# A decoder layer's FFN opening, its first norm and its buffer addresses rearranged

## The chip, the cores and the metric

The kernel runs on one core of a Trainium2 chip. The metric is device microseconds of one execution; lower is better. The core's engines run their own instruction streams side by side: TensorE (PE; its weight loads are listed as PEld), VectorE (DVE), ScalarE (ACT), GpSimd (POOL) and SyncE (SP, which issues most DMAs).

## The reference

One decoder layer over 512 tokens and 1024 channels, all in float32. Two token mixers work on the same input projection: gated linear attention (a) and sliding-window attention with sinks (b). Their outputs are projected, gated, added and projected by `w_out`; then come a post-norm, a SwiGLU FFN with 2816 hidden channels, and a second post-norm:

```python
def layer_norm(x, g, b):
    mu = jnp.mean(xf, axis=-1, keepdims=True)
    var = jnp.mean(jnp.square(xf - mu), axis=-1, keepdims=True)
    return (xf - mu) * lax.rsqrt(var + LN_EPS) * g + b
...
    merged = jax.nn.sigmoid(g_a) * y_a + jax.nn.sigmoid(g_b) * y_b
    return merged @ w_out
...
        h = layer_norm(DEEPNORM_ALPHA * h + mix, ln1_g[layer], ln1_b[layer])
        ffn = (jax.nn.silu(h @ w_gate) * (h @ w_up)) @ w_down
        h = layer_norm(DEEPNORM_ALPHA * h + ffn, ln2_g[layer], ln2_b[layer])
```

## The kernel before, in words

Every large product is made of three matmuls: each operand is split into a high part in the format fp32r and a low part, the remainder in the same format, and high x high, low x high and high x low are added in PSUM. For a weight, ACT casts the loaded block (`wh<-raw`) and DVE subtracts (`wl<-raw,wh`).

The program goes through these stages, with the times of the profiled execution: input, transposes and the first projections to 30 us; query, key, value and gate projections together with both attentions to 280 (`feat_tile`, line 227, and `gla_values`, line 421); the branch projections and gates to 460 (`pbb`, `pga`, `pba`, line 227); the first 512 columns of `w_out` to 482 (line 768), the second 512, one token tile of 128 after another in `out_half`, to 506 (line 779); norm 1 and the transposes of its result (`turned`, line 800); the FFN to 750; the down projection in two column halves to 876 (line 976); norm 2 and the stores to 885.

Tokens lie in four tiles of 128; `res[t][i]` is the residual of tile t in column half i. `norm_part` adds a result to the residual and takes its statistics. `norm_end` makes, on DVE, (x - mean) * g (line 739, two passes of 512 columns), the reciprocal root with one refining step, and times root plus b (line 751, two more).

The FFN's gate and up projection is one level of a Strassen-like scheme: 7 products in place of 8, for 11 pairs of 256 hidden channels (`i`), gate and up in turn (`n`). Each product ("seventh", line 894) is 12 matmuls of 128x256. The token-side operands are A11 and A12 (the first 256 tokens in two halves of the channels), A22 and the sums S1 to S4, which need all the tokens; `split_cols` (807 and 808) makes a high part on ACT and a low part on a given engine. A product b11 uses A11, b21 uses A12, t1 S1, t2 S2, t3 S3, b22 S4 and t4 A22. The profile calls A operands `a`, S1 to S4 `s`, the PSUM tiles of the products `fx`, `fy`, `fz`, and the weight-side sums `wb` and `wt`; the latter are prepared ahead by `prep_pairs` (ACT casts 880, DVE low parts 881, POOL sums 883 to 888).

The down projection reads for each of 22 hidden blocks `op`, the high and low part of the product act (`piece`, 968 and 969), from 10 buffers. In its second column half, the last 8 blocks are run token tile by token tile, so that each tile's `norm_end` can start when that tile is done.

Buffers come from pools that grow from both ends of SBUF. A pool on the right side ends at the same address and starts where its size puts it. Before, the right pools start at byte 196,576 of a partition (`xparts`: xh and xl, the split input; then `merged`: mh and ml, the split merged branches) or at 188,384 (`sums`: A22 and S1 to S4; then `halves`: op). All these addresses are 32 modulo 64. The tiles of the left pools (weights, A11, A12, and the branch outputs `obh`, `obl`, `oah`, `oal`) start at 0 modulo 64.

The order of the instructions on each engine is set when the program is built: a scheduler simulates the tile graph from the order of the code and issues what it takes to be ready. DMA queues are filled in program order by SP (most loads) and POOL (vectors and residuals).

## Time and profile before

| | us |
|---|---|
| median of 3 runs | 887.66 (887.15 to 888.57) |
| profiled execution | 886.88 |
| its span | 885.1 |
| PE busy | 849.0 (96%) |
| DVE busy | 582.9 (66%) |
| ACT busy | 402.4 (45%) |
| POOL busy | 259.9 (29%) |
| mean granted clock of TensorE | 0.982 |

The span is what the profile shows of the device; the execution's own time is 1.8 us longer. A row of a time line gives start, length, engine, line and operation, the tiles (written <- read), and in brackets the idle time before it with what ended it. Rows of grouped instructions give the count, busy time, mean in ns, and the idle time before them. Matmuls overlap: the distance from start to start, not the length, is what one costs.

### The profile page before, as it was taken

The page shows a single profiled execution, that of the slowest core. Times are in us where ns is not written, and L with a number is a line of the kernel's source. Part 1 is how long each engine was busy: PE and PEld are TensorE (multiplying, and loading weights), DVE is VectorE, ACT ScalarE, POOL GpSimd, SP SyncE. Part 2 cuts the span into 40 slices and gives each one's busy share as a digit, 9 for nine tenths or more (in the row PEclk, how much of TensorE's full clock was granted, in tenths as well). Part 3 has the DMA queues.
Part 4 walks back from the last instruction along what each step waited for, and adds up shares of the span by engine and source line. Part 5 has one row for each costly group of instructions (what it writes and reads, how often), then busy time and mean ns, then how long its engine had stood idle before and what let it go on. Part 6 is the DMA issues. An engine that isn't in the chain of part 4 may idle for free.

```text
span 885.1 us, 12931 instructions
## 1 busy us (share of the span) xinstructions
PE 849.0 (96%) x4922; PEld 729.6 (82%) x4922; DVE 582.9 (66%) x1052; ACT 402.4 (45%) x798; POOL 259.9 (29%) x216
## 2 busy tenths in 40 slices
PE   7999999999999999999999949999999999999995
PEld 6887777777887888888888739999999998788885
DVE  4898887686585533322444998888788789735337
ACT  4557566464553431122332345555554557433421
POOL 3240220112310220000232337555666652521201
PEclk9999999999999999999999968999999999999998
DMA  8423113122122323322229030334444314422202
GB/s 238 143 72 96 49 49 96 49 68 77 48 72 72 95 81 95 102 98 85 96 101 316 3 96 1 96 98 119 112 124 120 100 49 147 139 94 74 95 1 95
DMA packets 92622, 83.16 MB, mean 94 GB/s; under 512 B 4768, under 2 KB 79536, under 8 KB 92560
## 3 DMA queue, kind: packets, MB, share of 16 engines
q1 hardware_dynamic: 90480, 76.89, 29.8%
q0 software_dynamic: 1504, 4.40, 1.4%
q10 hardware_dynamic: 576, 1.05, 0.3%
q8 instruction: 38, 0.62, 0.3%
q14 instruction: 24, 0.20, 0.1%
HBM read 80.23 MB, written 2.10 MB: 93 GB/s over the span
## 4 chain that ended last, share of the span: by engine, by line
PE 68%; issue 13%; POOL 10%; DVE 6%; DMA 2%; ACT 1%; POOLq 0%; SPq 0%; DVEq 0%; ACTq 0%
PE pdn L976 12%; PE pva L421 5%; PE pgb L227 5%; PE pq L227 5%; PE pga L227 5%; PE pr L227 5%; PE pba L227 5%; PE pbb L227 5%; POOL upper L888 3%; POOL upper L885 3%; PE pka L227 3%; PE pw L768 3%; PE pqa L227 3%; POOL upper L886 2%; PE pw L779 2%
## 5 line engine op out<-in xcount | busy, mean ns | idle before, releaser
L160 DVE TENSOR_TENSOR wl<-raw,wh 128x1024 fp32r<-128x1024 f32 x96 | 121.1, 1262 | 147.2 <-ACT wh L159 146.9
L159 ACT CAST wh<-raw 128x1024 fp32r<-128x1024 f32 x96 | 100.5, 1049 | 140.4 <-PE pbb L227 34.3
L976 PE MATMUL pdn<-wh,op 128*128 128x512 f32 (+1 forms) x396 | 112.9, 370 | 2.5 <-ACT op L968 1.6
L881 DVE TENSOR_TENSOR wt<-upper,wt 128x512 fp32r<-128x512 f32 x88 | 77.6, 890 | 32.5 <-ACT wt L880 32.3
L880 ACT CAST wt<-upper 128x512 fp32r<-128x512 f32 x88 | 54.8, 624 | 75.4 <-POOL upper L885 37.2
L976 PEld LDWEIGHTS pdn<-wh,op 128*128 128x128 f32 x396 | 71.2, 188 | 17.5 <-ACT op L968 1.8
L976 PE MATMUL pdn<-wl,op 128*128 128x512 f32 (+1 forms) x198 | 73.2, 370 | 0.0
L894 PE MATMUL fx<-s,wt 128*128 128x256 f32 x528 | 65.9, 280 | 0.0
L894 PEld LDWEIGHTS fx<-s,wt 128*128 128x128 f32 x528 | 64.0, 189 | 0.0
L969 POOL TENSOR_TENSOR op<-act,op 128x512 fp32r<-128x512 f32 x22 | 29.2, 1337 | 81.8 <-ACT op L968 81.8
L883 POOL TENSOR_TENSOR upper<-upper 128x512 f32<-128x512 f32 x22 | 31.6, 1451 | 69.8 <-DVE wb L881 56.6
L695 POOL TENSOR_TENSOR ml<-gb,mh 128x512 fp32r<-128x512 f32 x8 | 11.4, 1423 | 119.7 <-ACT mh L694 119.7
L976 PEld LDWEIGHTS pdn<-wl,op 128*128 128x128 f32 x198 | 37.2, 188 | 6.9
L888 POOL TENSOR_TENSOR upper<-upper,lower 128x512 f32<-128x512 f32 x22 | 33.9, 1540 | 27.6 <-DVE wt L881 25.7
L881 DVE TENSOR_TENSOR wb<-lower,wb 128x512 fp32r<-128x512 f32 x44 | 40.2, 932 | 0.0
L968 ACT CAST op<-act 128x512 fp32r<-128x512 f32 x44 | 26.1, 617 | 25.9 <-PE pdn L976 24.4
L894 PE MATMUL fy<-s,wt 128*128 128x256 f32 x264 | 35.8, 294 | 1.9 <-ACT s L807 1.5
L886 POOL TENSOR_TENSOR upper<-upper,lower 128x512 f32<-128x512 f32 x22 | 36.9, 1695 | 0.1
L894 PEld LDWEIGHTS fy<-s,wt 128*128 128x128 f32 x264 | 34.3, 201 | 2.5 <-ACT s L807 1.9
L894 PE MATMUL fx<-a,wb 128*128 128x256 f32 x264 | 34.0, 283 | 1.1 <-DVE a L808 1.1
L377 ACT ACTIVATE S<-S,nm 128x256 f32<-128x256 f32 (+1 forms) x64 | 30.2, 476 | 10.1 <-DVE es L374 6.0
L894 PE MATMUL fx<-a,wt 128*128 128x256 f32 x264 | 33.5, 282 | 1.0 <-DVE gate L937 0.5
(485 smaller groups left out, 2222.2 us busy)
## 6 DMA issues: line engine op xcount, KB each, us to landing
raw<-in_w_in_dram SPq DMA_DIRECT2D x50, 512.0 KB, 3.7
raw<-in_w_ffn_down_dram SPq DMA_DIRECT2D x22, 512.0 KB, 3.5
upper<-in_w_ffn_gate_dram SPq DMA_DIRECT2D x22, 256.0 KB, 5.5
upper<-in_w_ffn_up_dram SPq DMA_DIRECT2D x22, 256.0 KB, 5.9
lower<-in_w_ffn_gate_dram SPq DMA_DIRECT2D x22, 256.0 KB, 4.9
lower<-in_w_ffn_up_dram SPq DMA_DIRECT2D x22, 256.0 KB, 3.4
raw<-in_w_branch_b_dram SPq DMA_DIRECT2D x8, 512.0 KB, 3.5
raw<-in_w_branch_a_dram SPq DMA_DIRECT2D x8, 512.0 KB, 3.4
```

The lines of the kernel that those rows point to most:

```text
L159: ACT.copy(wh, raw)
L160: DVE.tensor_tensor(wl, raw, wh.bitcast(F32), ALU.subtract)
L227: PE.matmul(ps[:, n0:n1], w, d[k][:, n0:n1] if isinstance(d, list) else d[:, k, n0:n1], start=i == 0, stop=i == 3 * NK - 1)
L377: ACT.activation(S[h], S[h], AF.Exp, bias=nm[:, h : h + 1], accum_out=den[:, h : h + 1])
L421: PE.matmul(pa[c], d[:, k, cs], w, start=k == 0 and i == 0, stop=k == NK - 1 and i == 2)
L880: ACT.copy(w[:, 0], src)
L881: DVE.tensor_tensor(w[:, 1], src, w[:, 0].bitcast(F32), ALU.subtract)
L883: POOL.tensor_tensor(b11, b11, b12, ALU.add)
L886: POOL.tensor_tensor(b12, b12, b22, ALU.add)
L888: POOL.tensor_tensor(b11, b11, b21, ALU.add)
L894: PE.matmul(ps, w[:, x, k * P : (k + 1) * P], op[:, y, k, :], start=start and i == 0, stop=stop and i == len(todo) - 1, skip_group_check=True)
L976: PE.matmul(ps[:, c0:c1], op[:, x, ts], w[y][:, c0:c1], start=start and n == 0, stop=stop and n == 2)
```

## The change

It has five parts.

1. A tile of 32 bytes per partition, `edge`, is put at the outer end of the right side. All right pools now start at 0 modulo 64.
2. `norm_rows` replaces `norm_end` in norm 1: ACT makes (x - mean) * root in two passes, without gain and shift. These are two columns (`lncol`, loaded on POOL's queue at the start) and are applied to the transposed result by `affine`, ACT or DVE, in steps of 128 columns. The residual itself gets them later, by 16 POOL passes (`gain`) in the first half of the down projection; the row vectors g1 and b1 are loaded at the end of the FFN, beside g2 and b2, and no longer before norm 1.
3. The FFN opens with pairs 0 and 1 together: b11 of both, b21 of both, t1 of both and so on. The products that use only the first 256 tokens are then 8, or 96 matmuls, where there were 4. `last_tokens` and `last_sums` make S1 first and the other sums afterwards. Pairs are prepared already between the token tiles of `out_half`; their weights use buffers freed by placing three of the blocks of `w_out` in `four` tiles. The tiles fz move to the other PSUM group.
4. S1, S2 and S3 get a pool of their own, freed after the last pair's t3. The pool `halves` takes its place, with 6 `op` buffers instead of 10, and the first pieces are made before the FFN ends. The low parts of the first column half's pieces are all made by DVE.
5. `wide` has 6 buffers, `four` 11, and the last pair's results share one tile.

```diff
+    edge = tc.alloc_tile_pool(name="edge", bufs=1, side="right")
+    edge.tile([P, 8], F32, tag="edge", name="edge")
     right = phase("xparts", "right")
...
+    for c, v in zip(lncol, (ln1_g, ln1_b)):
+        nc.gpsimd.dma_start(c, v[0].rearrange("(k p) -> p k", p=P))
...
-    gains = [four(n) for n in ("g1", "b1")]
-    for g, v in zip(gains, (ln1_g, ln1_b)):
-        nc.gpsimd.dma_start(g, v.broadcast_to([P, D]))
...
+    def norm_rows(t, stats, name):
+        mv = stat(f"mv{name}{t}", 2)
+        DVE.bn_aggr(mv, stats)
+        y, v, w = stat(f"y{name}{t}", 1), stat(f"v{name}{t}", 1), stat(f"w{name}{t}", 1)
+        ACT.activation(y, mv[:, 1:2], AF.Sqrt, bias=eps)
+        DVE.tensor_scalar(v, mv[:, 1:2], LN_EPS, None, ALU.add)
+        refine(y, v, w)
+        DVE.tensor_scalar(w, mv[:, 0:1], y, -1.0, ALU.mult, ALU.mult)
+        for i in (1, 0):
+            ACT.activation(res[t][i], res[t][i], AF.Identity, bias=w, scale=y)
...
+    def affine(eng, h, cs, pt, kg):
+        for k in range(HK):
+            g, b = [c[:, HK * kg + k : HK * kg + k + 1] for c in lncol]
+            if eng is ACT:
+                ACT.activation(h[:, k, cs], pt[:, k, :], AF.Identity, bias=b, scale=g)
+            else:
+                DVE.tensor_scalar(h[:, k, cs], pt[:, k, :], g, b, ALU.mult, ALU.add)
...
+    def last_tokens(t):
+        cs = slice((t - 2) * P, (t - 1) * P)
+        p22, p21 = turned(t, 1), turned(t, 0)
+        affine(ACT, h22, cs, p22, 1)
+        affine(DVE, s3, cs, p21, 0)
+        DVE.tensor_tensor(s1[:, :, cs], s3[:, :, cs], h22[:, :, cs], ALU.subtract)
         split_cols(S1, cs, s1[:, :, cs], DVE)
...
+    groups = [[0, 1]] + [[i] for i in range(2, HF)]
+    flow = []
+    for grp in groups:
+        order = ORDER if len(grp) == 1 else ["b11", "b21", "t1", "t2", "t3", "b22", "t4"]
+        flow += [(i, q, n) for q in order for i in grp for n in range(2)]
...
+    for t in range(2):
+        out_half(t)
+        norm_rows(t, st1[t][:, 0:2, :], "a")
+        prep_pairs(2 + 2 * t)
+        if t:
+            first_tokens(0)
...
     right.release()
-    right = phase("halves", "right")
+    right = phase("sums", "right")
+    A22, S4 = [operand(right, n) for n in ("a22", "s4")]
+    right2 = phase("sums2", "right")
+    S1, S2, S3 = [operand(right2, n) for n in ("s1", "s2", "s3")]
...
+        if i == done:
+            right2.release()
+            right2 = phase("halves", "right")
...
+                    op = right2.tile([P, 2, T], F32R, tag="op", name=f"op{j}_{k}", bufs=6)
+                    ACT.copy(op[:, 0], act[k])
+                    (POOL if j and k % 2 else DVE).tensor_tensor(op[:, 1], act[k], op[:, 0].bitcast(F32), ALU.subtract)
...
+            for k in range(4):
+                piece(0, k)
...
-            op = right.tile([P, 2, T], F32R, tag="op", name=f"op{j}_{k}", bufs=10)
-            ACT.copy(op[:, 0], act[k])
-            (POOL, DVE)[k % 2].tensor_tensor(op[:, 1], act[k], op[:, 0].bitcast(F32), ALU.subtract)
...
+    g1, b1 = vec_bcast(ln1_g, tail, "g1"), vec_bcast(ln1_b, tail, "b1")
     g2, b2 = vec_bcast(ln2_g, tail, "g2"), vec_bcast(ln2_b, tail, "b2")
...
+        if gain:
+            r, v, op = gain.pop(0)
+            POOL.tensor_tensor(r, r, v, op)
```

The orders below are those of the built programs. A row has the line, the operation, the tile written <- the tiles read with their numbers, the shape, and how often it stands there in a row.

PE before, where the FFN opens: 48 matmuls on A11 and A12 (the last rows of them are shown), then the transposes of token tiles 2 and 3, then t1 on S1.

```order
L894 MATMUL fx_0_4555<-a_4277,wb_0_4575 128x256 x11
L894 MATMUL fx_1_4556<-a_4277,wb_1_4579 128x256 x11
L894 MATMUL fz_0_4559<-a_4278,wb_0_4641 128x256
L894 MATMUL fz_1_4560<-a_4278,wb_1_4644 128x256 x2
L894 MATMUL fz_0_4559<-a_4278,wb_0_4641 128x256 x10
L894 MATMUL fz_1_4560<-a_4278,wb_1_4644 128x256 x10
L800 MATMUL pt_h_1_4478<-ident,res_1_4121 128x128 x4
L800 MATMUL pt_h_0_4485<-ident,res_0_4120 128x128 x4
L800 MATMUL pt_h_1_4518<-ident,res_1_4123 128x128 x4
L800 MATMUL pt_h_0_4525<-ident,res_0_4122 128x128 x4
L894 MATMUL fy_0_4557<-s_4471,wt_0_4595 128x256
L894 MATMUL fy_1_4558<-s_4471,wt_1_4614 128x256
```

PE after, the same place:

```order
L819 MATMUL pt_h_1_4582<-ident,res_1_4129 128x128 x4
L921 MATMUL fx_0_4552<-a_4281,wb_0_4350 128x256 x11
L921 MATMUL fx_1_4567<-a_4281,wb_1_4354 128x256 x11
L819 MATMUL pt_h_0_4587<-ident,res_0_4128 128x128 x4
L921 MATMUL fx_0_4605<-a_4281,wb_0_4399 128x256 x11
L921 MATMUL fx_1_4620<-a_4281,wb_1_4403 128x256 x11
L819 MATMUL pt_h_1_4635<-ident,res_1_4131 128x128 x4
L819 MATMUL pt_h_0_4640<-ident,res_0_4130 128x128 x4
L921 MATMUL fz_0_4659<-a_4282,wb_0_4656 128x256 x12
L921 MATMUL fz_1_4676<-a_4282,wb_1_4673 128x256 x12
L921 MATMUL fz_0_4693<-a_4282,wb_0_4690 128x256 x12
L921 MATMUL fz_1_4710<-a_4282,wb_1_4707 128x256 x12
```

The transposes have moved in among the first products, and four groups of fz, of both pairs, stand behind the last of them and ahead of the first on S1.

DVE after, from the last token tile's shift (L839 is `affine` on DVE, L908 a weight's low part, L859 and L857 `last_sums`, L965 an FFN result) to the low part of S1 (s_4542) for that tile, which is its last row:

```order
L852 TENSOR_TENSOR s1f<-s3f,h_4545 128x4x128
L965 TENSOR_TENSOR act_0_4550<-fz_1_4676,u_01_4580 128x256
L827 TENSOR_TENSOR s_4542<-s1f,s_4542 128x4x128
L908 TENSOR_TENSOR wt_0_4786<-upper_0_4338,wt_0_4786 128x512
L827 TENSOR_TENSOR a_4537<-h_4545,a_4537 128x4x128
L965 TENSOR_TENSOR gate_0_4603<-fz_0_4693,u_10_4618 128x256
L908 TENSOR_TENSOR wt_1_4790<-upper_1_4344,wt_1_4790 128x512
L859 TENSOR_TENSOR s3f<-h_4283,s3f 128x4x128
L965 TENSOR_TENSOR act_0_4550<-fz_1_4710,u_11_4633 128x256
L857 TENSOR_TENSOR s1f<-s1f,h_4283 128x4x128
L908 TENSOR_TENSOR wt_0_4794<-upper_0_4326,wt_0_4794 128x512
L827 TENSOR_TENSOR s_4542<-s1f,s_4542 128x4x128
```

Between the last tile's difference (its L852 row, the first) and that low part stand weight preparations and results of both pairs; before, the four passes L739 and L751 of the last tile stood ahead of it instead.

PE before, in the second half of the down projection, where token tile 0 (pdn_0_0) is finished and tile 1 follows:

```order
L976 MATMUL pdn_0_0_7927<-wh_8184,op_19_8258 128x512 x2
L976 MATMUL pdn_0_0_7927<-wl_8185,op_19_8258 128x512
L976 MATMUL pdn_0_0_7927<-wh_8224,op_20_8264 128x512 x2
L976 MATMUL pdn_0_0_7927<-wl_8225,op_20_8264 128x512
L976 MATMUL pdn_0_0_7927<-wh_8224,op_21_8270 128x512 x2
L976 MATMUL pdn_0_0_7927<-wl_8225,op_21_8270 128x512
L976 MATMUL pdn_1_0_7928<-wh_8100,op_14_8228 128x512 x2
L976 MATMUL pdn_1_0_7928<-wl_8101,op_14_8228 128x512
```

PE after, the last rows of the program:

```order
L1045 MATMUL pdn_3_1_7979<-wh_8272,op_21_8318 128x256
L1045 MATMUL pdn_0_0_7975<-wh_8272,op_21_8318 128x512
L1045 MATMUL pdn_0_0_7975<-wl_8273,op_21_8318 128x512
L1045 MATMUL pdn_1_0_7976<-wh_8272,op_21_8318 128x512
L1045 MATMUL pdn_1_0_7976<-wl_8273,op_21_8318 128x512
L1045 MATMUL pdn_2_0_7977<-wh_8272,op_21_8318 128x512
L1045 MATMUL pdn_2_0_7977<-wl_8273,op_21_8318 128x512
L1045 MATMUL pdn_3_0_7978<-wh_8272,op_21_8318 128x256
L1045 MATMUL pdn_3_0_7978<-wl_8273,op_21_8318 128x256
L1045 MATMUL pdn_3_1_7979<-wh_8272,op_21_8318 128x256
L1045 MATMUL pdn_3_1_7979<-wl_8273,op_21_8318 128x256
```

With 6 buffers, blocks 20 and 21 stand behind blocks 14 to 19 of all four token tiles, and the last block is run for all the tiles in turn.

More of the change, by code (lines that the diff above doesn't have):

```diff
@@ L142, in tile_decoder_layer @@
     NRAW = 3
-    raws, ready = [], []
+    raws, ready, homes = [], [], {}
     def fetch_to(n):
@@ L191, in tile_decoder_layer @@
     gng = const.tile([P, 2], F32, tag="gng", name="gng")
+    lncol = [const.tile([P, NK], F32, tag=f"lncol{i}", name=f"lncol{i}") for i in range(2)]
     sink = const.tile([P, 16], F32, tag="sink", name="sink")
@@ L704, in four @@
     def four(name, dt=F32):
-        return late.tile([P, 1024], dt, tag="four", name=name, bufs=12)
+        return late.tile([P, 1024], dt, tag="four", name=name, bufs=11)
+    first_wo = index["wo", 1][0]
+    for i in range(first_wo + 1, first_wo + 4):
+        homes[i] = four
     def vec_bcast(v, home, tag):
@@ L895, in seventh @@
                       stop=stop and i == len(todo) - 1, skip_group_check=True)
-    act = [[None] * HF for _ in range(2)]
-    act_pairs = [[four(f"act{h}_{p}").rearrange("p (k t) -> p k t", k=2) for p in range((HF + 1) // 2)]
-                 for h in range(2)]
     T0, T1 = slice(0, HT), slice(HT, T)
@@ L957, in tile_decoder_layer @@
     limit[0] = len(units)
[L960 removed]
+    g1, b1 = vec_bcast(ln1_g, tail, "g1"), vec_bcast(ln1_b, tail, "b1")
     g2, b2 = vec_bcast(ln2_g, tail, "g2"), vec_bcast(ln2_b, tail, "b2")
     st2 = new_stats("b")
[L963 to L971 removed]
+    gain = [(r, v[i], op) for t in range(NT) for i, r in enumerate(res[t]) for v, op in ((g1, ALU.mult), (b1, ALU.add))]
     def down(k, t, ps, w, op, start, stop, c0=0, c1=512):
```

172 lines of the change are left out of this document (93 added, 79 removed).

## The prediction

> **What bounds the kernel now.** I read the stretch table first, then the chain, the shapes on TensorE, and the time lines of the places that the change touches. The stretch table gives for each stretch its length, the busy time of PE, PEld, DVE, ACT and POOL, and the granted clock.
>
> ```profile
> 30.00:280.00 250.00, 248.54 (x1295) 196.26 (x1294) 192.64 (x491) 138.83 (x340) 50.27 (x46) 1.00 0.25 70
> 328.00:460.00 132.00, 132.00 (x578) 108.13 (x577) 45.32 (x49) 34.79 (x42) 13.28 (x9) 1.00 0.31 95
> 506.00:549.00 43.00, 28.36 (x191) 26.46 (x190) 38.65 (x58) 23.31 (x44) 22.97 (x15) 0.76 0.19 50
> 549.00:750.00 201.00, 199.53 (x1677) 198.51 (x1675) 168.43 (x241) 111.75 (x238) 107.71 (x73) 1.00 0.37 103
> 750.00:876.00 126.00, 124.08 (x594) 102.27 (x594) 64.49 (x87) 45.90 (x68) 30.79 (x25) 1.00 0.25 84
> 876.00:885.10 9.10, 0.00 (x0) 0.00 (x0) 4.94 (x12) 0.82 (x3) 3.11 (x3) 0.61 0.31 115
> ```
>
> TensorE is the bound in all but two stretches: 506 to 549 (norm 1 into the FFN: DVE 38.65 of 43, PE 28.36 at a clock of 0.76) and the tail after 876. So the change can act in four ways: on the rate of single matmuls, on that transition, on the FFN's end, and on the tail. The chain (start, length) shows the first:
>
> ```profile
> 327.95 43.55 PE pbb L227 x192
> 371.49 44.80 PE pga L227 x192
> 416.30 43.56 PE pba L227 x192
> 459.86 22.39 PE pw L768 x96
> ```
>
> All are 128x512 matmuls without a gap. pbb and pba read oh/ol, at 0 mod 64 bytes: 43.55/192 = 226.8 ns. pga reads xh/xl and pw reads mh/ml, which the program puts at 32 mod 64: 44.80/192 = 233.3 and 22.39/96 = 233.2 ns. The weights are the same kind of tile in all four.
>
> **Part 1, the aligned pools.** By shape (count, busy us, mean ns; the mean overlaps with the next matmul, so only differences count):
>
> ```profile
> L227 PE MATMUL pga<-xh,wh 128*128 128x512 f32 x64 | 25.3, 395 | 0.0
> L227 PE MATMUL pba<-oah,wh 128*128 128x512 f32 x64 | 24.9, 389 | 0.0
> L894 PE MATMUL fx<-s,wt 128*128 128x256 f32 x528 | 65.9, 280 | 0.0
> L894 PE MATMUL fx<-a,wb 128*128 128x256 f32 x264 | 34.0, 283 | 1.1 <-DVE a L808 1.1
> L976 PE MATMUL pdn<-wh,op 128*128 128x512 f32 x308 | 97.4, 396 | 2.5 <-ACT op L968 1.6 <-POOL op L969 0.5 <-DVE op L969 0.4
> ```
>
> pdn (396 ns) stands with pga: op too is at 32. 512-wide matmuls with one operand at 32: 960 of L227, 192 of pva, 192 of pw, 462 of pdn, 1806 in all. At 6.5 ns each (233.3 − 226.8) that is 11.7 us. The 256-wide ones go the other way: those on A11/A12 (`a`, 0 mod 64) take 283 ns, those on S1 to S4 (32) 280. So 5/7 of the FFN's 1848 matmuls, 1320, could lose about 2 ns: +2.6 us, and some 390 more 256-wide ones (pk, pv, pd, the last tile of pdn) +0.7. Net −8.4. In 30 to 280 PE idles 1.46 of 250 us on DVE and ACT, so a little of the gain there turns into waits: I take −8 (bounds 0, if address is not what separates the rows, and −11.7, if the FFN loses nothing).
>
> The Trainium skill, "TensorE: Matmul & The Clock Gate", section "Wait — 56ns, not 53.3ns?", gives a warm matmul as N ÷ 2.4 GHz + 2.5 ns, 215.7 ns at N = 512, with no term for an address; by it this part would be 0. The trace has two values for one shape, 226.8 and 233.3, so I follow the trace; the page's case is rival A.
>
> **Part 2, the transition.** Before, on PE and then on DVE:
>
> ```profile
> 506.94 0.39 PE L894 MATMUL fz<-a,wb 128*128 128x256 f32 x1 [0.33 <-ACT wb L880]
> 508.40 2.90 PE L894 MATMUL fx<-a,wb 128*128 128x256 f32 x22 [1.08 <-DVE a L808]
> 517.63 1.94 PE L800 MATMUL pt_h<-ident,res 128*128 128x128 f32 x8 [3.58 <-DVE res L751]
> 527.00 1.94 PE L800 MATMUL pt_h<-ident,res 128*128 128x128 f32 x8 [7.42 <-DVE res L751]
> 530.44 0.80 PE L894 MATMUL fy<-s,wt 128*128 128x256 f32 x2 [1.50 <-ACT s L807]
> 531.59 5.06 PE L894 MATMUL fy<-s,wt 128*128 128x256 f32 x22 [0.35 <-DVE s L808]
> 536.45 3.08 PE L894 MATMUL fx<-s,wt 128*128 128x256 f32 x24
> 504.59 1.77 DVE L739 SCALAR_TENSOR_TENSOR res<-res,mva,g 128x512 f32<-128x512 f32 x1
> 518.02 0.74 DVE L739 SCALAR_TENSOR_TENSOR res<-res,mva,g 128x512 f32<-128x512 f32 x1
> 522.00 1.57 DVE L808 TENSOR_TENSOR s<-s1f,s 128x512 fp32r<-128x512 f32 x1
> 530.85 0.69 DVE L808 TENSOR_TENSOR s<-s1f,s 128x512 fp32r<-128x512 f32 x1
> ```
>
> The 191 PE instructions of 506 to 549 are 175 FFN matmuls at 2.90/22 to 3.08/24, say 0.12 us pitch (21), and 16 transposes (1.6): 22.6. So 43 − 22.6 = 20.4 us are lost: 14.3 in the waits shown, the rest at half clock (22 fy take 5.06, 24 fx afterwards 3.08).
>
> After, 16 DVE passes (L739, L751) go. ACT gets 8 passes of 512 wide and 24 steps of 128 wide that apply gain and shift to pt_h, and loses 6 copies of pt_h (ACT and POOL of 482 to 549):
>
> ```profile
> L807 ACT CAST s<-s1f 128x512 fp32r<-128x512 f32 x4 | 2.5, 617 | 6.1 <-DVE s1f L838 5.0 <-DVE s1f L835 1.2
> L819 ACT COPY h<-pt_h 128x512 f32<-128x512 f32 x4 | 2.2, 590 | 0.4 <-DVE a L808 0.4
> L841 POOL TENSOR_TENSOR h<-h,s1f 128x512 f32<-128x512 f32 x2 | 2.5, 1274 | 2.0 <-DVE ya L495 1.4 <-DVE s1f L838 0.6
> ```
>
> 8 × 0.62, 24 × some 0.3 and −6 × 0.59 add 8.6 us to ACT's 23.31 of 43: it stays behind DVE, so they cost nothing of their own, and each pair of h and S waits 0.6 longer than on a copy (4 × 0.3 against 0.59), which the estimate below holds. PE has 96 matmuls (11.5 us) that need no S, against 48. DVE gets work in front: four wb preparations of pairs 0 and 1 stand before the first norm parts. In its new order 33 DVE rows lie from the last token tile's L733 to the second low half of S1: 20 of 512 wide at a pitch of 0.60, 4 of 256 at 0.33, 8 of 128 at some 0.24, and six tiny (1.3): 16.5 us. That L733 is at 509.05 before; counted with the inserted rows and the passes saved ahead of it, it stays near 509.3. S1 is then whole at 525.8, or 528.5 if four or five of the rows run at POOL's mercy (1.57 and 1.77 against 0.69 and 0.74 above). PE has done its 96 by about 521.4: second wo half to 506.2, 11.5 of matmuls, 1.7 of transposes, and 0.7 + 1.2 of waits for A11 and pt_h. One wait of 4.7 to 7.4 stays, I take 6.0, with about 2.5 of half clock behind it (half of what stood behind 7.42), and 1 of small ones. Lost: 0.7 + 1.2 + 6.0 + 2.5 + 1.0 = 11.4 against 20.4, so −9 (bounds −13, if the wait ends short of any clock drop, and +1, all DVE rows slow).
>
> The same page, section "What's actually happening", says that the clock halves after an idle window of about 3.4 us. The trace agrees: slow transposes and matmuls stand behind waits of 3.58 and 7.42. By that rule a wait shortened under 3.4 us would save 2.5 us more than its length; I forecast 6.0, so it is not reached.
>
> The two gain passes per half tile move to POOL in the first down half: 16 at 1.27 (L841) to some 1.5 us, 22; POOL is busy 30.79 of 126 there. Nobody waits for them before norm 2: cost nothing; without that cover they would cost all 22. The 1 MB of g1/b1 leaves 470 and joins the FFN's end, where DMA is at 0.25 to 0.37: nothing. Two column loads of 1,024 4-byte elements each join the start on POOL's queue, like these, among the x loads for which PE waits:
>
> ```profile
> bdec<-in_b_decay_dram POOLq DMA_DIRECT2D x1, 2.0 KB, 6.3
> ```
>
> 512 such elements landed in the usual 6 us; two of 1,024 can cost between 0 and 1.5 us of those queues, I take +0.8.
>
> **Part 3, the FFN's steady state** (PE 199.53 of 201) stays: same matmuls, only Part 1. **Part 4, its end:** the pdn row shows 2.5 us of waits on op; with its pieces made ahead in freed space, and edges, −3 (bounds 0 and −3.3).
>
> **Part 5, the tail.** Each token tile ends with a norm on DVE, beside PE's next tile:
>
> ```profile
> 875.49 0.27 PE L976 MATMUL pdn<-wl,op 128*128 128x256 f32 x1
> 858.93 0.69 DVE L725 SCALAR_TENSOR_TENSOR res<-res,pdn 128x512 f32<-128x512 f32 x1 [8.40 <-PE pdn L976]
> 864.53 0.69 DVE L725 SCALAR_TENSOR_TENSOR res<-res,pdn 128x512 f32<-128x512 f32 x1 [0.21 <-PE pdn L976]
> 870.13 0.69 DVE L725 SCALAR_TENSOR_TENSOR res<-res,pdn 128x512 f32<-128x512 f32 x1 [0.22 <-PE pdn L976]
> 875.81 0.42 DVE L725 SCALAR_TENSOR_TENSOR res<-res,pdn 128x256 f32<-128x256 f32 x1 [1.16 <-PE pdn L976]
> 880.04 1.15 DVE L751 SCALAR_TENSOR_TENSOR res<-res,yb,b 128x256 f32<-128x256 f32 x2
> 858.00:885.10 27.10, 17.77 (x100) 15.22 (x98) 19.76 (x48) 3.02 (x7) 3.63 (x3) 0.87 0.21 78
> ```
>
> Tiles finish 5.6 us apart, and DVE ends at 881.2, 5.7 after the last matmul. The tiles' four runs need op 14 to 21 whole; after, there are 6 slots, so op 20 and 21 reuse those of 14 and 15 and can be written only when the last tile has read these. PE's new order ends with op 20 for all tiles, then op 21 for all tiles: they finish within about 1.5 us. DVE then has four tiles at once: 19.76 us busy (20.7 from 858.93 to 881.2 less the waits), less 1 to 2 where one tile's tiny steps fill another's, from 1.1 before the last matmul: an end 16.4 to 19.6 behind it instead of 5.7. I take +12 (10.7 to 13.9).
>
> **Sum:** −8 − 9 + 0.8 − 3 + 12 = −7.2. The profiled execution took 886.88 (span 885.1); that gives 879.7. The median shown is 0.8 above it: 880.4.
>
> **Rivals.** A: addresses make no difference, and pga and pba differ by something else that stays. For it: the 256-wide rows go the other way, so "aligned" isn't simply better. Against: four uniform blocks separate exactly by address. −9 + 0.8 − 3 + 12: 888.4, no change. The Trainium skill, "SBUF — State Buffer", section "Operand start alignment", asks of an address only a multiple of the element size, and says its runs timed nothing; no run here shows that rule.
>
> B, slower: S1 comes later still. Place: the 20 wide DVE rows ahead of S1's second low half. If nearly all of them ran at 1.2 instead of 0.6 us beside POOL's sums for pair 1, S1 would come 10 us later: 890.5. It decides once S1 is whole 9 us later than I put it, about 535 on the old clock. For it: DVE is busy 38.65 of 43 and POOL 22.97. Against: only some rows of that stretch read over 1 us.
>
> C: the tail costs half, +6, because ACT and POOL take their shares early and DVE's tiny steps vanish, or the wait for S1 shrinks under the clock drop: 872 to 874. For it: ACT is busy 0.82 of 9.10 there. Against: only two of the four tiles hand a share aside.
>
> **How the numbers follow.** Forecast (875 to 885.5) 0.62; C and the like 0.13; A 0.06; B 0.13; a forecast off by a little into no change 0.06. A difference of under 0.2%, 1.8 us, can't be told from none: faster 0.75, same 0.11, slower 0.14. The range reaches from 872 (C) to 889, which leaves B and the far end of C out.
>
> **What would show it.** Aligned: pga and pw at 227 ns pitch, fx<-s near 283. Transition: one wait of 4.7 to 7.4 at the first fy, none above 2 on pt_h. FFN's end: pdn waits under 0.5. Tail: four L733 rows within 2 us of the last matmul and DVE busy 17 us or more after it. I am wrong if pga stays at 233, if PE waits over 10 us for S1, or if the tail after the last matmul is under 15 us in all (9.6 before).

## The result and the profile after

The changed kernel takes 909.97 us (median of 4 runs, 909.68 to 911.0) against 887.47 (887.15 to 888.57) in the same series: a ratio of 1.0253, 95% interval 1.0236 to 1.0271. It is 22.5 us slower; 880.4 was forecast, in a range of 872 to 889, with 0.14 on slower. The profiled execution has a span of 909.3 us against 885.1, 24.2 more. Where these stand, from the starts of PE's first and last matmuls of each stage:

| us after minus before | shift |
|---|---|
| up to the end of `w_out` | −1.35 |
| transition and first pairs | −0.65 |
| steady pairs of the FFN | 0 |
| end of the FFN, up to the first down matmul | +17.1 |
| down projection | −3.4 |
| from the last matmul to the end | +12.4 |

The stretch table of after (length, then busy time of PE, PEld, DVE, ACT and POOL, then the granted clock, the busy share of the DMA engines and GB/s) shows the transition, the FFN's end, the down projection and the tail:

```profile
505.00:548.00 43.00, 30.44 (x210) 28.96 (x210) 35.27 (x56) 25.99 (x56) 23.89 (x14) 0.80 0.08 22
741.00:768.00 27.00, 9.97 (x60) 9.39 (x59) 26.05 (x14) 8.76 (x14) 18.42 (x16) 0.68 0.28 97
766.00:888.00 122.00, 121.54 (x595) 102.21 (x593) 51.51 (x63) 41.09 (x58) 18.53 (x11) 1.00 0.22 70
887.50:909.30 21.80, 0.04 (x1) 0.00 (x0) 17.56 (x46) 2.91 (x7) 4.07 (x3) 0.60 0.25 97
```

The second row is new: 27 us in which PE works 9.97 and DVE seems busy for 26.05, with only 14 instructions. DVE's time line there (start, length) shows one of them:

```profile
741.95 18.56 DVE L165 TENSOR_TENSOR wl<-raw,wh 128x1024 fp32r<-128x1024 f32 x1 [1.88 <-ACT wh L164]
760.43 0.41 DVE L968 TENSOR_TENSOR gate<-q,fx 128x256 f32<-128x256 f32 x1
```

POOL's time line of the same moment:

```profile
738.71 0.53 POOL L721 DMA_DIRECT2D g<-in_ln_g_dram  x1 [4.77 <-PE fz L921]
739.22 0.53 POOL L721 DMA_DIRECT2D b<-in_ln_b_dram  x1
739.77 9.91 POOL L1054 TENSOR_TENSOR res<-res,g 128x512 f32<-128x512 f32 x8
749.65 9.78 POOL L1054 TENSOR_TENSOR res<-res,b 128x512 f32<-128x512 f32 x8
```

And PE's:

```profile
760.90 5.16 PE L921 MATMUL fx<-a,wt 128*128 128x256 f32 x24 [17.03 <-DVE gate L968]
```

A subtraction that takes 1.21 us elsewhere (738.19 on the same time line) takes 18.56. It arrives in the second of POOL's 16 gain passes and ends at 760.5, 1.1 us after the last one (749.65 + 9.78 = 759.4): it stands still for the burst and then takes about its usual time. The gate result behind it on DVE frees the PSUM tile for PE's last product, so PE waits 17.03 and then runs 24 matmuls at a granted clock that is still 0.50 up to 763, 5.16 in place of 2.88.

The chain of after answers the question on addresses:

```profile
327.42 43.55 PE pbb L233 x192
370.97 44.80 PE pga L233 x192
415.77 43.55 PE pba L233 x192
```

The groups by shape add the down projection and the S products (busy us, mean ns, waits):

```profile
L1045 PE MATMUL pdn<-wh,op 128*128 128x512 f32 x308 | 95.6, 392 | 0.0
L921 PE MATMUL fx<-s,wt 128*128 128x256 f32 x528 | 63.1, 276 | 0.0
```

pga stays at 233.3 ns a matmul, although all pools are at 0 modulo 64 now. pdn has gone from 396 to 392 and has no waits; fx<-s has become faster (280 to 276), where 283 was forecast. The transition, PE's time line:

```profile
507.10 0.95 PE L921 MATMUL fx<-a,wb 128*128 128x256 f32 x4 [2.08 <-ACT a L826]
...
524.14 0.50 PE L921 MATMUL fy<-s,wt 128*128 128x256 f32 x2 [1.05 <-ACT s L826]
527.86 0.58 PE L921 MATMUL fy<-s,wt 128*128 128x256 f32 x1 [3.23 <-DVE gate L965]
530.14 0.58 PE L921 MATMUL fy<-s,wt 128*128 128x256 f32 x1 [1.69 <-DVE act L965]
534.83 7.80 PE L921 MATMUL fy<-s,wt 128*128 128x256 f32 x44 [4.11 <-DVE s L827]
```

DVE's time line at the same place, from the last tile's difference to the last low part of S1:

```profile
520.97 1.45 DVE L852 TENSOR_TENSOR s1f<-s3f,h 128x512 f32<-128x512 f32 x1
...
533.02 1.75 DVE L827 TENSOR_TENSOR s<-s1f,s 128x512 fp32r<-128x512 f32 x1
```

S1's last low part ends at 534.8, where 525.8 to 528.5 was forecast. Between 520.97 and 534.8, eight rows of 512 read 1.42 to 1.75 us in place of 0.69. POOL is busy beside all of them, with weight sums and, from 525.2 on, also with low parts and sums of the other operands. DVE also sat idle for 3.00 us before the last two token tiles' shifts (513.86), until `pt_h` was there. The tail, PE's last row:

```profile
887.26 0.28 PE L1045 MATMUL pdn<-wl,op 128*128 128x256 f32 x1
```

DVE's first and last rows of norm 2:

```profile
886.19 1.29 DVE L733 SCALAR_TENSOR_TENSOR res<-res,pdn 128x512 f32<-128x512 f32 x2 [4.58 <-PE pdn L1045]
...
904.23 1.15 DVE L770 SCALAR_TENSOR_TENSOR res<-res,yb,b 128x256 f32<-128x256 f32 x2
```

Four tiles finish together, and DVE ends 18 us after the last matmul.

### The profile page after: what moved, and what is told of

The parts are those of the page before. It is cut to its first block, busy times and chain, and to the rows that moved or that the text cites. A ratio compares the mean times of both kernels' runs of the same rounds, so it can differ in the third digit from the quotient of the medians.

```text
span 909.3 us, 12952 instructions
## 1 busy us (share of the span) xinstructions
PE 844.4 (93%) x4922; PEld 727.5 (80%) x4922; DVE 592.7 (65%) x1059; ACT 411.9 (45%) x824; POOL 276.3 (30%) x223
## 3 DMA queue, kind: packets, MB, share of 16 engines
q10 hardware_dynamic: 576, 1.05, 0.3%
## 4 chain that ended last, share of the span: by engine, by line
PE 65%; issue 13%; POOL 9%; DVE 7%; DMA 4%; ACT 1%; SPq 1%; POOLq 0%; DVEq 0%; ACTq 0%
PE pdn L1045 13%; PE pgb L233 5%; PE pq L233 5%; PE pr L233 5%; PE pga L233 5%; PE pva L429 5%; PE pba L233 5%; PE pbb L233 5%; POOL upper L915 3%; POOL upper L913 3%; PE pka L233 2%; POOL upper L912 2%; PE pqa L233 2%; PE fx L921 2%; PE po L410 2%
## 5 line engine op out<-in xcount | busy, mean ns | idle before, releaser
L165 DVE TENSOR_TENSOR wl<-raw,wh 128x1024 fp32r<-128x1024 f32 x96 | 138.7, 1446 | 117.2 <-ACT wh L164 116.8
L1045 PE MATMUL pdn<-wh,op 128*128 128x512 f32 (+1 forms) x396 | 110.8, 367 | 0.0
L908 DVE TENSOR_TENSOR wt<-upper,wt 128x512 fp32r<-128x512 f32 x88 | 77.5, 889 | 31.2 <-ACT wt L907 31.0
L1045 PEld LDWEIGHTS pdn<-wh,op 128*128 128x128 f32 x396 | 71.2, 188 | 12.4
L921 PE MATMUL fx<-s,wt 128*128 128x256 f32 x528 | 63.1, 276 | 0.0
L921 PEld LDWEIGHTS fx<-s,wt 128*128 128x128 f32 x528 | 61.5, 188 | 0.0
L921 PEld LDWEIGHTS fx<-a,wt 128*128 128x128 f32 x264 | 33.0, 199 | 23.5 <-DVE gate L968 23.5
L1026 POOL TENSOR_TENSOR op<-act,op 128x512 fp32r<-128x512 f32 x11 | 18.5, 1685 | 104.8 <-ACT op L1025 104.8
L1026 DVE TENSOR_TENSOR op<-act,op 128x512 fp32r<-128x512 f32 x33 | 23.5, 720 | 33.5 <-ACT op L1025 33.5
L908 DVE TENSOR_TENSOR wb<-lower,wb 128x512 fp32r<-128x512 f32 x44 | 39.4, 911 | 3.1 <-ACT wb L907 3.1
L915 POOL TENSOR_TENSOR upper<-upper,lower 128x512 f32<-128x512 f32 x22 | 33.9, 1544 | 23.6 <-DVE wt L908 23.6
L912 POOL TENSOR_TENSOR upper<-upper,lower 128x512 f32<-128x512 f32 x22 | 33.1, 1522 | 25.1 <-DVE wt L908 25.1
```

Of the source, the lines that this page charges most:

```text
L165: DVE.tensor_tensor(wl, raw, wh.bitcast(F32), ALU.subtract)
L908: DVE.tensor_tensor(w[:, 1], src, w[:, 0].bitcast(F32), ALU.subtract)
L912: POOL.tensor_tensor(b11, b11, b22, ALU.add)
L915: POOL.tensor_tensor(b11, b11, b21, ALU.add)
L921: PE.matmul(ps, w[:, x, k * P : (k + 1) * P], op[:, y, k, :], start=start and i == 0, stop=stop and i == len(todo) - 1, skip_group_check=True)
L1026: (POOL if j and k % 2 else DVE).tensor_tensor(op[:, 1], act[k], op[:, 0].bitcast(F32), ALU.subtract)
```

## The experiments

Theory 1 was, after this reading: the +17 is POOL's burst keeping DVE from its operands; the +12 is the 8 blocks run tile by tile with 6 buffers; x stays at 233 by an address rule other than alignment to 64. Ratios are to runs of the kernel before in the same series (887.2, 886.9, 887.1, 887.4 and 887.5).

**The gain passes.** `no_gain` leaves the loop out, `gain_eight` keeps the 8 multiplications, and `gain_spread` issues the 16 in twos behind later low parts. Its low parts of even blocks are on POOL again, and the four loads come there behind three of these, at 748.9 to 751.0:

```diff
...
-        if gain:
-            r, v, op = gain.pop(0)
-            POOL.tensor_tensor(r, r, v, op)
+        if k >= 6 and k % 2 == 0:
+            with tc.issue_after(lows[0, k].ins):
+                for r, v, op in gain[k - 6 : k - 4]:
+                    POOL.tensor_tensor(r, r, v, op)
```

> The changed kernel with the 16 GpSimd passes that apply gain and shift to the residual left out (so norm 2 works on a residual without them). Theory 1: these passes, back to back from 739.8 to 759.4, keep VectorE's one subtraction waiting for 18.6 us and through it the last pair's t3 result, so the FFN's end comes 17 us sooner: 893 +- 2 us, and the wait of 17.0 before fx<-a,wt in the last pair falls under 1. Theory 2: that wait is for the loads at this place (2 MB of gain and shift rows beside the down weights): the time stays at 908 to 911.

> The changed kernel with all 16 passes kept, but queued on GpSimd in twos behind the low parts of op 6, 8, ... 20 of the first down half (those low parts of even blocks are on GpSimd again, as before the change). Theory 1: no burst, so the 17 us go as without the passes, and at most 1 to 2 us come back as short VectorE waits in the down half: 893 to 895. Theory 2 (the loads): 908 to 911. Theory 3 (any pass on GpSimd beside VectorE costs its own length, in a burst or not): 16 x 1.25 = 20 us of VectorE waits come back in the down half, but VectorE has 59 of 109 us idle there, so this theory too gives at most 897.

> The changed kernel with the 8 multiplying gain passes kept where they are and the 8 adding ones left out (norm 2 then works on a residual without the shift). Theory 1 (VectorE gets in only when the burst ends): the subtraction there takes about 8.8 us and the wait before the last fx<-a,wt about 7: 899 to 901. Theory 2 (it gets in once some number of passes is over, or something else at that place holds it): 890 or 908 to 910.

`no_gain` took 889.38 (ratio 1.0023, 1.0012 to 1.0034), `gain_spread` 889.04 (1.0014, 1.0001 to 1.0027): 20.6 and 20.9 less than after, and 2 to 6 less than their Theory 1 gave. In `no_gain` all four loads are issued at the same place as in after and the wait is gone, so theory 2 is out. So nearly the whole loss of the FFN's end, and the half clock behind it, goes with the burst as it stands there and not with the passes themselves. PE's time line of `gain_spread` has no wait there:

```profile
743.58 2.88 PE L921 MATMUL fx<-a,wt 128*128 128x256 f32 x24
```

`gain_eight` took 899.68 (1.0126, 1.0104 to 1.0149). With half the burst the subtraction takes half as long, as DVE's time line of this kernel shows:

```profile
742.30 9.00 DVE L165 TENSOR_TENSOR wl<-raw,wh 128x1024 fp32r<-128x1024 f32 x1 [1.77 <-ACT wh L164]
```

It ends at 751.3, again 1.1 us after POOL's burst:

```profile
740.31 9.90 POOL L1054 TENSOR_TENSOR res<-res,g 128x512 f32<-128x512 f32 x8
```

**Why for the whole burst.** Two measurements by themselves, `port_bench` (7 bursts of 16 POOL passes on various tiles) and `port_phase` (6 bursts of 12, DVE arriving in the second pass or later), had DVE subtract beside them.

> A kernel that computes none of the reference: seven times a burst of 16 GpSimd passes of 128x512, and in the midst of it two VectorE subtractions with two SBUF inputs, 512 or 1024 wide in turn: passes to another tile, passes in place, and passes with one input in place. In the changed kernel one subtraction of 1024 stood still for the whole burst (18.6 us), while elsewhere each waited for one pass. Theory 1 (passes in place don't let VectorE in): 20 us for VectorE's first subtraction beside passes in place, 1.2 to 1.8 beside the others. Theory 2 (the width of VectorE's operation decides): 20 us wherever it is 1024 wide. Theory 3 (neither; the state of the queues at that place decides): 1.2 to 2.2 everywhere.

> A kernel that computes none of the reference: six bursts of 12 GpSimd passes of 128x512, beside each two VectorE subtractions, 1024 or 512 wide, that arrive in the second pass or later; five bursts of passes that wait for nothing (the fifth in place), one (the fourth) whose passes have a met wait on GpSimd's own earlier passes. Theory 1 (an operation that arrives in the second or a later pass of a run without waits is shut out to its end): 10 us or more for the first subtraction of each burst but the fourth. Theory 2 (VectorE always gets the next turn; the kernel's case has another condition): 1.2 to 2.2 us in all.

Neither reproduced it: the first subtraction took 1.13 to 2.29 us, the next of 1024 up to 2.17. What the kernel has and these had not is loads issued by POOL just ahead. `loads_behind` is the changed kernel with g2 and b2 loaded behind the burst; `loads_bench` adds such loads to the bursts.

```diff
-    g2, b2 = vec_bcast(ln2_g, tail, "g2"), vec_bcast(ln2_b, tail, "b2")
...
-            POOL.tensor_tensor(r, r, v, op)
+            last = POOL.tensor_tensor(r, r, v, op)
+    with tc.issue_after(last.ins):
+        g2, b2 = vec_bcast(ln2_g, tail, "g2"), vec_bcast(ln2_b, tail, "b2")
```

> The changed kernel, but the loads of g2 and b2 on POOL's queue are issued behind the 16 gain passes instead of ahead of them, so that no transfer that POOL issued is under way when DVE's subtraction arrives in the burst. Theory 1: transfers issued by POOL that are still landing are what keeps DVE from getting a turn between two passes. Then the subtraction takes about 2 us instead of 18.56, the wait ahead of the last products shrinks from 17 to about 1, and the time is 889 to 893. Theory 2: the burst alone does it, whatever is loading: again 17 to 19 us and 909 to 911.

> Not the layer: six bursts of 16 unwaited POOL passes of 512, with two DVE subtractions of 1024 that arrive in the second pass or later. Bursts 1 and 6 have no transfer under way; bursts 2 and 3 follow two loads of 512 KB issued by POOL, bursts 4 and 5 run beside two such loads issued by SP. Theory 1 (loads by POOL shut DVE out): in bursts 2 and 3 the first subtraction lasts to the burst's end, 14 to 20 us; in 1, 4, 5 and 6 1.1 to 2.3. Theory 2 (the burst alone, for a reason that the kernel has and this bench has not): 1.1 to 2.3 in all six. A third: any load into SBUF does it, then also in bursts 4 and 5.

`loads_behind` took 894.81 (1.0081, 1.0061 to 1.0101): 15.2 less than after, with all 16 passes in one burst, though 2 more than its Theory 1 allowed. DVE's time line there:

```profile
741.54 1.66 DVE L165 TENSOR_TENSOR wl<-raw,wh 128x1024 fp32r<-128x1024 f32 x1
743.12 3.48 DVE L1026 TENSOR_TENSOR op<-act,op 128x512 fp32r<-128x512 f32 x2
```

POOL's, from the second load's issue:

```profile
731.44 0.54 POOL L721 DMA_DIRECT2D b<-in_ln_b_dram  x1
735.13 16.03 POOL L1053 TENSOR_TENSOR res<-res,g 128x512 f32<-128x512 f32 x8 [3.15 <-DMA g<-in_ln_g_dram]
```

The engines now take turns: DVE is slowed to 1.7 us an operation, POOL to 2.0. What is left against `gain_spread`, 5.8 us, is mostly that: PE waits 4.0 us once for op in the down projection. In `loads_bench`, bursts 1 and 6 have no loads, 2 and 3 have loads by POOL ahead, 4 and 5 loads by SP; the first subtraction of 1, 2 and 4 on DVE's time line:

```profile
9.03 1.80 DVE L102 TENSOR_TENSOR low<-one,two 128x1024 fp32r<-128x1024 f32 x1 [9.03 <-ACT one L101]
...
34.35 18.68 DVE L102 TENSOR_TENSOR low<-one,two 128x1024 fp32r<-128x1024 f32 x1 [4.84 <-ACT one L101]
...
88.38 1.90 DVE L102 TENSOR_TENSOR low<-one,two 128x1024 fp32r<-128x1024 f32 x1 [4.90 <-ACT one L101]
```

Bursts 2 and 3 (18.68 and 17.89) reproduce the kernel's 18.56; 5 and 6 (1.27 and 1.23) share like 1 and 4. `loads_when` asked what of it decides:

> Not the layer: five bursts of 16 POOL passes, each behind loads issued by POOL, with two DVE subtractions of 1024. Burst 1: two loads of 512 KB, DVE arrives about 3 us after the issue, while they land. Burst 2: the same, DVE arrives 11 us after the issue, when they have landed, in the middle of the burst. Burst 3: the first pass waits for the second load, DVE arrives in the second pass. Burst 4: one load. Burst 5: two loads of 8 columns. Theory 1 (a load that POOL issued and that is under way at the moment when DVE arrives shuts it out): to the burst's end in 1 and 4, about 2 us in 2 and 3. Theory 2 (a burst that starts without a wait behind POOL's issue is not shared, whenever DVE comes): to the burst's end in 1, 2, 4 and 5, about 2 us in 3. The size of the load: if only long transfers matter, burst 5 shares.

The first subtraction in bursts 1, 2, 3 and 5, on DVE's time line:

```profile
11.25 18.75 DVE L98 TENSOR_TENSOR low<-one,two 128x1024 fp32r<-128x1024 f32 x1 [11.25 <-ACT one L97]
...
46.86 10.11 DVE L98 TENSOR_TENSOR low<-one,two 128x1024 fp32r<-128x1024 f32 x1 [13.35 <-ACT one L97]
...
69.91 1.46 DVE L98 TENSOR_TENSOR low<-one,two 128x1024 fp32r<-128x1024 f32 x1 [9.44 <-ACT one L97]
...
122.83 18.53 DVE L98 TENSOR_TENSOR low<-one,two 128x1024 fp32r<-128x1024 f32 x1 [4.90 <-ACT one L97]
```

POOL's time line at the start of bursts 2 and 3:

```profile
35.76 0.53 POOL L88 DMA_DIRECT2D bb<-in_ln_b_dram  x1
36.30 1.27 POOL L90 TENSOR_TENSOR row<-key,gain 128x512 f32<-128x512 f32 x1
37.53 18.35 POOL L93 TENSOR_TENSOR row<-key,gain 128x512 f32<-128x512 f32 x15
...
67.80 1.26 POOL L90 TENSOR_TENSOR row<-key,bb 128x512 f32<-128x512 f32 x1 [4.56 <-DMA bb<-in_ln_b_dram]
```

Theory 2 of that run holds. In burst 1 and in burst 4, behind one load, DVE is shut out to the end (18.75 and 18.54). In burst 2 DVE arrives at 46.86, 11 us after an issue whose load lands in about 5, and still waits for the burst's end (10.11). In burst 3 the first pass waits for the load, and DVE shares (1.46). In burst 5 the loads are of 4 KB, and it is shut out as well (18.53). So a POOL burst that starts without a wait behind POOL's own DMA issue isn't shared with DVE, and one that starts with a wait is. That the loads are still landing when the burst begins doesn't decide it: in `loads_behind` the second load was issued at 731.44 and landed 4.8 us later, after the first pass at 735.13, and DVE shared. Two things stay open. In every burst that was shared, the first pass had waited for something, in those without POOL's loads for a copy by ACT; so no run has a burst with neither a wait nor an issue ahead. And whether the wait itself or the 3.2 to 4.6 us between issue and first pass decides, no run separates. What inside POOL does this, none shows either.

The Trainium skill, "SBUF — State Buffer", section "Who interferes with whom", says that a DVE instruction with two SBUF inputs contends with a GpSimd instruction that reads SBUF. The Trainium skill, "SBUF — State Buffer", section "SBUF: two separate sides", says that whichever of the two starts first has the shared ports for its whole instruction. The alternation above agrees (1.21 us becomes 2.17). That a whole run of instructions can shut DVE out is in neither section; 18.56 us shows it here. The second half of `address_bench`, described below, fits too: four DVE additions with two SBUF inputs took 6.20 to 6.32 us beside POOL passes and 2.87 without them, four statistics passes with one input 2.88 beside them. (Its four with an input in PSUM ran after their burst and show nothing; in after, such a row, `gate<-fz,u`, takes 0.41 beside POOL at 527.39 and 0.41 at 739.33 without POOL's passes.)

**The tail.** `split_six` runs only the last 6 blocks tile by tile, as many as there are buffers:

```diff
-    split = NF - 8
+    split = NF - 6
```

> The changed kernel with the last 6 blocks instead of 8 run token tile by token tile in the second down half, so that 6 op buffers hold them all. Theory 1: the tail grew by 12.4 us since tiles end together; now they end 4.2 us apart, VectorE's norm of 5.4 per tile falls 1.2 a tile behind, and the tail costs 2 to 4 us instead of 12.4: 900 to 902. Rival: the tail is long because the vectors of norm 2 or ScalarE's and GpSimd's shares come late, whatever the order of the blocks: 908 to 911.

`split_six` took 899.82 (1.0138, 1.0119 to 1.0156): 10.2 less than after, of which 7.8 lies behind the last matmul (14.2 in place of 22.0). Another 2.1 stands ahead of the down projection (its first matmul starts at 763.8 in place of 765.9), which this edit doesn't touch; that part is not explained. With buffers for all 8 blocks, in `all_four` below, the tail is back at 9.6.

**Addresses.** `edge_only` is the kernel before with the 32-byte tile alone; `pad_left` is after with 64 bytes more in the constants, which moves the left pools.

```diff
+    edge = tc.alloc_tile_pool(name="edge", bufs=1, side="right")
+    edge.tile([P, 8], F32, tag="edge", name="edge")
```
```diff
+    shift = const.tile([P, 16], F32, tag="shift", name="shift")
```

> The kernel before with nothing but the 32-byte tile at the outer end of the right side; the order of the instructions on TensorE is the same. Theory 1 (only an operand that is loaded as weights from the right side, or the S operands of the FFN, is sped up; x as the moving operand stays at 233 ns): pva, pw and pdn save 3 to 4 ns each on some 850 matmuls, 3 us; the FFN's matmuls fall from 118 to 113.5 ns but its pairs stay at 20.3 us each, since VectorE and GpSimd set that: 884.0 to 885.0. Theory 2 (every faster matmul counts): 9 us for the FFN more: 875 to 877. Theory 3 (the rates of the changed kernel come from its other order): 887.5.

> The changed kernel with one unused 64-byte tile more in the pool of constants, which moves every left pool by 64 bytes, to 64 modulo 128, where the right pools stand. Theory 1 (a matmul's pitch depends on the distance of its two operands' addresses modulo 128, and the change undid its own alignment, since the two new gain columns move the left pools by 64): pga and all other matmuls on x fall from 233 to 227 ns (960 x 6.4 = 6.1 us), pva, pw and pdn save 2 to 3 ns more (2 us), the FFN's S matmuls rise from 113.5 to 120 ns without a cost, since the pairs stay at 20.3 us: 901 to 903. Theory 2 (64-byte alignment of each tile for itself, and the 233 ns comes from the new order): 910.

`edge_only` took 879.58 (0.9908, 0.9892 to 0.9924), 7.6 less than before, between its theories 1 (884 to 885) and 2 (875 to 877). Neither had the mechanism: in its chain pga, which theory 1 left at 233, joins the others:

```profile
323.52 43.57 PE pbb L229 x192
367.08 43.52 PE pga L229 x192
```

`pad_left` took 913.94 (1.0298, 1.0284 to 1.0312), 4 more than after: a miss. `address_bench` then ran 48 matmuls each at chosen offsets.

> A kernel that computes none of the reference: blocks of 48 matmuls, each with a new stationary operand, 128x512 (long) and 128x256 (half), where the moving operand (m) and the stationary one (s) start 0, 32, 64 or 96 bytes (a, b, c, d) behind a 128-byte boundary, or 128, 256, 512, 1024, 192, 320 bytes further (e to j). Theory 1 (distance modulo 128): 227 and 120 ns wherever both letters are equal, whichever they are, 233 and 113 to 118 where they differ; e to h as a, i and j as c. Theory 2 (each for itself): rates that depend on one letter alone. Behind it, four equal VectorE operations beside eight GpSimd passes of two SBUF inputs, 128x512: with two SBUF inputs on VectorE, Theory 1 (shut out until the burst ends) has one of them take about 10 us; with one input from PSUM, or one input at all, 0.7 us each. If VectorE only shares, each takes 1.3 to 1.8.

On PE's time line the blocks follow each other, so the distance of two starts is the price of 48 (md, mf, mi and mj move the moving operand by 96, 256, 192 and 320 bytes against the stationary one; "half" is 256 wide):

```profile
155.74 11.36 PE L80 MATMUL long_md_sa<-big 128*128 128x512 f32 x48
166.94 11.15 PE L80 MATMUL long_md_sb<-big 128*128 128x512 f32 x48
...
211.21 11.06 PE L80 MATMUL long_mf_sa<-big 128*128 128x512 f32 x48
222.10 11.04 PE L80 MATMUL long_mg_sa<-big 128*128 128x512 f32 x48
...
243.86 11.36 PE L80 MATMUL long_mi_sa<-big 128*128 128x512 f32 x48
255.06 11.16 PE L80 MATMUL long_mj_sa<-big 128*128 128x512 f32 x48
266.06 11.30 PE L80 MATMUL long_ma_se<-big 128*128 128x512 f32 x48
...
299.61 5.82 PE L80 MATMUL half_ma_sc<-big 128*128 128x256 f32 x48
305.26 5.79 PE L80 MATMUL half_ma_sd<-big 128*128 128x256 f32 x48
...
402.05 5.62 PE L80 MATMUL half_mi_sa<-big 128*128 128x256 f32 x48
407.51 5.82 PE L80 MATMUL half_mj_sa<-big 128*128 128x256 f32 x48
```

+96 costs (166.94 − 155.74)/48 = 233.3 ns, +256 226.9, +192 233.3 and +320 229.2; 256 wide, +192 costs 113.8, where equal offsets gave 119.7 to 120. At 512 wide all 24 blocks go by the distance from the stationary to the moving operand modulo 256, not by the alignment of either (128 gave 233.3 in one direction and 231.9 in the other). At 256 wide that is not the whole rule: ma_sc, a distance of −64, leaves the same remainder as +192 and costs (305.26 − 299.61)/48 = 117.7, so the 113.8 stands on one block and on the kernel's own S products. Worked out from the programs' addresses, the right pools lie 32 from the left ones before, 0 in `edge_only` and 192 in after, since the two gain columns (2 x 32 bytes in the constants) move all left pools by 64. That gives 233 for x, 229 for pdn (there the stationary operand is the one on the right, so the distance is 64) and 113.8 for the S products, which start 114.2 apart in after's steady pairs; in `pad_left` the distance is 128, 233 again and without the gain on S.

**The transition.** `open_first` puts the other sums and the weights for later products behind S1 on DVE:

```diff
+            with tc.issue_after(whole[3].ins) if q not in ("b11", "b21", "t1") and i < 2 else nullcontext():
                 DVE.tensor_tensor(w[:, 1], src, w[:, 0].bitcast(F32), ALU.subtract)
...
+        with tc.issue_after(whole[3].ins):
             last_sums(t)
```

> The changed kernel with VectorE's work for the FFN's start in another order: the low parts of the weights from t2 on and the sums S2, S3 of both last token tiles stand behind the last low part of S1 and no longer ahead of it (11 rows less ahead). Theory 1 (VectorE's order makes S1 late): S1 is whole 7 us sooner, at 527 to 529 instead of 535, the three waits of 3.2, 1.7 and 4.1 us shrink to 3 in all, and the half clock behind them goes: 900 to 903. Theory 2 (GpSimd's passes take VectorE's time at this place whatever the order): S1 at 533 or later, or the wait comes back at S2: 907 to 910.

`open_first` took 911.47 (1.0272, 1.0258 to 1.0286). S1 comes in time, and S2 is late in its place, as theory 2 had it, on PE's time line:

```profile
525.64 1.64 PE L922 MATMUL fy<-s,wt 128*128 128x256 f32 x12 [0.54 <-DVE act L966]
534.96 1.22 PE L922 MATMUL fx<-s,wt 128*128 128x256 f32 x4 [7.68 <-ACT s L826]
542.34 9.84 PE L922 MATMUL fx<-s,wt 128*128 128x256 f32 x59 [6.16 <-DVE s L827]
```

**Together.** `all_four` has `pad_left`, `open_first`, `gain_spread` and separate buffers for the last 8 blocks' pieces; `three_mends` has the spread passes, those buffers and a pad of 192 bytes, which makes all pools equal modulo 256. `one_pair` is `three_mends` with the FFN opened by pair 0 alone, `no_sums` is `three_mends` without POOL's weight sums for pairs 0 and 1.

```diff
+    shift = const.tile([P, 48], F32, tag="shift", name="shift")
...
-                    op = right2.tile([P, 2, T], F32R, tag="op", name=f"op{j}_{k}", bufs=6)
+                    late_ = j and k >= NF - 8
+                    op = (tail if late_ else right2).tile([P, 2, T], F32R, tag="opt" if late_ else "op", name=f"op{j}_{k}", bufs=8 if late_ else 6)
```

> The changed kernel with four mends together: the 64-byte pad, VectorE's other order at the FFN's start, the gain passes spread over the first down half, and the last eight op pieces of the second down half in buffers of their own in the room that the FFN leaves (so that the token tiles end apart again). If the parts add up: 910 - 8 - 7 - 21 - 12 = 862; since a faster part may only uncover another wait, 860 to 870. If the mends hide behind each other (the pad's gain is lost to VectorE, or S1's wait comes back as a wait for S2): 872 to 880.

> The changed kernel with three mends: gain passes spread over the first down half; the last eight op pieces of the second down half in buffers of their own; and an unused tile of 192 bytes among the constants, so that all left and right pools stand at the same distance modulo 256 (the 64-byte pad left them 128 apart). Theory 1 (a matmul's pitch follows the distance of its operands modulo 256): pga, pr, pq at 227, pw and pdn at 227, S and A matmuls at 120, 6 to 8 us less than with the two other mends alone; 889.0 - 12.4 (tail) - 7 = 868 to 871. Theory 2 (the address has nothing to do with it): 875 to 878.

> As the kernel with three mends, but the FFN opens with pair 0 alone, as before the change (b11, b21, t1 and so on); the first norm without gain and shift, the early weight sums and all else stay. Theory 1 (VectorE's work sets the transition, and a second pair only brings its work for pair 1 forward, ahead of S1): the same within 2 us of the two-pair version. Theory 2 (the two-pair opening covers the wait for S1 with 5.7 us of matmuls, as I had it): 5 us slower.

> As the kernel with three mends, with GpSimd's sums for the weights of pairs 0 and 1 left out (those products then use unsummed weights). Theory 1 (beside these sums each VectorE operation of two SBUF inputs waits for a GpSimd pass, about 1 us each on 8 rows): VectorE's rows ahead of S1 fall from 1.4 to 1.8 us to 0.7, S1 is whole 6 to 8 us sooner, 6 to 9 us less in all. Theory 2 (VectorE's amount of work alone, or ScalarE's columns, set it): at most 2 us less.

`all_four` took 886.3 (0.9988, 0.9979 to 0.9996), above both of its ranges, its tail 9.6 again. `three_mends` took 877.16 (0.9896, 0.9881 to 0.9911). That is in the range of its theory 2, but its rates are those of theory 1: pga costs 43.52/192 = 226.7 ns. In the profiled executions the faster matmuls bring 3.9 us by the end of `w_out` against after, and the first down matmul starts only 2.2 earlier than in `gain_spread`, the nearest kernel without the pad; the rest is not accounted for. `one_pair` took 876.78 (0.9877, 0.986 to 0.9895): opening with two pairs brings nothing that can be measured. `no_sums` took 871.56 (0.9825, 0.9805 to 0.9846), 5.6 less than `three_mends`, a little short of the 6 to 9 of its theory 1: about that much of the transition is POOL's sums slowing DVE. Five of the eight slow rows read 0.68 or 0.69 there, and S1's last low part ends at 526.5 instead of 531.4; the other three rows still stand beside POOL's low parts and sums of the other operands. `three_mends` and `one_pair`, 1.0 and 1.2% under before, are the fastest that compute the whole layer; `edge_only`, with one tile of 32 bytes, comes within 2.4 us of `three_mends`.

## Why the prediction was wrong

- **The step that failed: "Nobody waits for them before norm 2: cost nothing"** (Part 2, the gain passes). I looked for readers of the passes' results and found none. The price fell on DVE, which reads none of them: its next instruction, a subtraction with two SBUF inputs, was kept out to the burst's end, and PE waited behind it. The cover I named, POOL's idle time, was there; I didn't ask what DVE does beside a burst. Measured, the passes cost 20.6 us (`no_gain`), as a burst and not by their number (`gain_spread`, 20.9 less with all 16). On PE's time line 17.03 of it is the wait and 2.28 the half clock behind it. "Without that cover they would cost all 22" gave the right size, for another reason. The rows of before held half the hint, 1.57 against 0.69 beside POOL, and I used it at S1 only; that a burst shuts DVE out whole, no row of before shows.
- **Part 1, −8:** near for the edge tile in before's layout (−7.6, `edge_only`), partly by luck: up to the end of `w_out` and in the down projection it brought −6.9 and −2.1 where some −11 was forecast, but between the two, in transition and FFN, it lost 0.6 and not 2.6. It is wrong in after: −1.35 up to the FFN and some 2 in the down projection. The step that failed is the reading of four blocks by each operand's own address, 0 or 32 modulo 64. Distance modulo 256 explains the same four blocks, and I did not count what else the change adds to the left side. Rival A, no difference by address, is wrong as well.
- **Part 2, transition, −9:** −0.65. The 8 rows beside POOL's passes cost 12.7 us in place of 5.5, where I allowed four or five at about 1.2, and DVE's idle 3.00 before `pt_h` was not in my count of rows at all (which says 33, while its own parts add up to 38; the 16.5 us come from the parts). The first of these rows, L733, stood at 506.94, 2.4 earlier than I put it. The one wait of 4.7 to 7.4 became four, of 1.05, 3.23, 1.69 and 4.11. This is rival B's mechanism, on 8 rows where it took nearly all 20: S1 at 534.8, next to its decision point of 535.
- **Column loads, +0.8:** nothing of that size shows. The first matmul of pq starts at 28.40 us before and at 28.47 after; no run leaves the loads out.
- **Part 3:** the steady pairs keep their period, 20.3 us; the S products are faster and the time went into waits on the gate results.
- **Part 4, −3:** right; pdn's waits are gone, 2.5 to 0.0. 1.6 of them stood before its first matmul and so lower the +17.1 of the table; of the −3.4 of the down projection, some 1.9 is the faster pitch, which belongs to Part 1.
- **Part 5, +12:** right: +12.4, DVE's last row ends 18 us after the last matmul; `split_six` and `all_four` show the cause, the order that 6 buffers force on the last blocks. Rival C is wrong.

The sum with the measured terms is −1.35 − 0.65 + 17.1 − 3.4 + 12.4 = 24.1, against 24.2 of span.
